# Two more pairs of gate chunks by seven products, and the turn of the merged sums moved behind them

## The chip, the cores and the metric

The kernel runs on one core of one Trainium2 chip. The metric is the device time of one execution in microseconds; for the kernel before it is 2109.54 us, the median of three runs (2108.2 to 2111.12).

## What is computed

Two transformer-like blocks follow each other on 256 tokens of width 2048, in float32. The change lies in the first block, behind its four attention branches. With `x` normalised to `h`, and `p = h @ w_in`, each branch b has a part `z_b` (512 columns) and a gate `g_b` (2048 columns) of `p`:

```
for b in range(4):
    y = branches[b] * silu(z_parts[b])                    # 256 x 512
    term = sigmoid(g_parts[b]) * (y @ w_branch[b])        # 256 x 2048
    merged = term if merged is None else merged + term
x = x + merged @ w_out                                    # the output projection
```

So there are 16 chunks of gates (four branches, four chunks of 512 columns), each a product of h (256 x 2048) with a 2048 x 512 block of `w_in`, and 16 products of y (256 x 512) with a 512 x 512 block of `w_branch`. Then the merged sums, turned, go into four chunks of the output projection.

## The kernel before, in words

**Products.** Every number is split into a high and a low part of 32 bits with a short mantissa, and a product of two numbers is three products on TensorE: high times low, high times high, low times high (`product`, L248 to L252; in the pairs L344). Every product instruction is 128 x 128 by 128 x 512, and adds up in a bank of PSUM.

**Units.** The work is a list of units (`self.units`). A unit is one load of 1 MB of weights (four blocks of 128 rows by 512 columns) with what is done with it: 24 product instructions for a plain unit (four blocks, two halves of the tokens, three products). A chunk of gates is four such units, a branch product is one. `run_units` (L279) writes the program out in order: for unit j it issues the conversion (ScalarE casts the load to `hi`, L317; VectorE subtracts to get `lo`, L318), then the products of unit q = j - 2 with what closes them, then it calls `pump`, then the loads that have become possible. `hi` and `lo` have three buffers, so the cast for unit q + 2 goes into the buffer of unit q - 1. A unit marked `late` has its conversion behind the products of unit q.

**Helpers.** Smaller work is in lists of generators: `pump` (L192) makes one step of the first generator of the list `fast` and of the first of `slow`, once per unit. A generator has to be at the head of its list to be stepped. A unit that needs a result calls `need`, which finishes the generators of that list up to the one named, on the spot. Turning a 256 x 512 part of the sums is such a helper:

```
    def turn_gen(self, src, k0, dst, scale=None):
        yield
        self.turn(src, 4, k0, dst(), scale)
```

Its first step does nothing; the second issues eight transposes on TensorE (L491), and for each of two banks a cast on ScalarE (L507) and a subtraction on VectorE (L508), which give the high and the low part. Unit gi of each chunk of the output projection needs turn ("m", gi).

**Pairs.** Two chunks of gates can go as a pair (`pair_units`, L329): the first eight blocks of x and the two weights are taken as 2 x 2 blocks, and seven products of sums of blocks take the place of eight; the last eight blocks go in plain units (l0, l1, r0, r1). The sums of weight blocks are added by VectorE in the loads' own buffers (L298), and the sums of x's blocks are made once (`forms_of`, L458, two steps, each two additions, four differences, four casts and four subtractions). `weave` puts pairs behind each other in the order of `GATE_PLAN`; r0 and r1 belong to the pair before (for the first pair they are the last two units of the chunk before), and bl and br are the two branch units of the pair before:

```
    order=("P1", "r0", "r1", "P5", "bl", "P6", "P3", "P7", "l0", "Q4", "l1", "P2", "br"),
```

Before, chunk (0,0) and chunk (0,1) go one by one, then five pairs hold (0,2) to (2,3), and the four chunks of branch 3 go one by one, each with a branch unit of an earlier chunk behind its first unit or behind itself. At the end stand branch units (3,2) and (3,3), and then the output projection.

**Places.** At the end of chunk (0,0) `to_merge` (L1006) closes the attention's pools and opens those of the merge, also `pS`, which holds the sums of x's blocks and two more buffers for loads. With the first unit of chunk (0,1) `fresh` (L922) reopens the banks of PSUM as five and three in place of four and four (`banks`, L593) and queues the sums of x's blocks. With the first unit of chunk (3,0) `to_sums` (L1018) closes `pS` and puts the turned sums `mT` in its place; `windows` tells the planner of loads between which units the two more buffers exist. At the end of branch unit (3,c) the turn ("m", c) is queued (L898).

Of the kernel before, what the change touches and what calls it, by code (L numbers as in the profile page):

```python
# [9 lines left out]
F32 = mybir.dt.float32  # L10
# [7 lines left out]
P = 128  # L18
# [3 lines left out]
NB = 4  # L22
BW = 512
FF = 5632
CH = 512
# [150 lines left out]
class Kernel:  # L176
# [413 lines left out]
            self.right.close()  # L590
            self.ps.close()

    def banks(self, n):  # L593

        if n != 4:
            self.ps.close()
        self.ps = ExitStack()
        self.psM = self.ps.enter_context(self.tc.tile_pool(name="psM", bufs=n, space=PSUM))
        self.psA = self.ps.enter_context(self.tc.tile_pool(name="psA", bufs=8 - n, space=PSUM))

    def start(self):

# [157 lines left out]
    def first_block_units(self):  # L760
# [112 lines left out]
        def g_evac(b, c):  # L873
            def evac(ps):
                if (b, c) == (0, 0):
                    self.to_merge()
                for m in range(2):
                    s = sig[b, c, m] = self.p2.tile([P, CH], F32, tag="sig", name="sig", bufs=4)
                    nc.scalar.activation(out=s, in_=ps[m], func=AF.Sigmoid, scale=self.r0(m))
                if (b, c) == (0, 0):  # L880
                    for i in range(2):
                        self.add(self.y_turn(i), name=("y", i))

            return evac

        def b_evac(b, c):
            def evac(ps):
                for m in range(2):
                    r = self.R[:, m, c * CH : (c + 1) * CH]
                    if b == 0:  # L890
                        nc.vector.tensor_tensor(out=r, in0=ps[m], in1=sig[b, c, m], op=ALU.mult)
                    else:
                        t = self.p2.tile([P, CH], F32, tag="tm", name="tm", bufs=2)
                        nc.vector.tensor_tensor(out=t, in0=ps[m], in1=sig[b, c, m], op=ALU.mult)  # L894
                        nc.vector.tensor_tensor(out=r, in0=r, in1=t, op=ALU.add)
                if c == 3 and b < 2:
                    self.add(self.y_turn(b + 2), name=("y", b + 2))
                if b == 3:  # L898
                    self.add(self.turn_gen(lambda m: self.R[:, m, c * CH : (c + 1) * CH], 4 * c, lambda: self.mT), name=("m", c))

            return evac

# [5 lines left out]
        def gate(b, c, fresh=None):  # L908
            return self.gemm(wg(b, c), kx, xl, g_evac(b, c), fresh=fresh)

        def branch(b, c):
            return self.gemm(wb[b, c], k4, lambda: self.yT[b], b_evac(b, c), need=lambda gi: ("y", b), add=False, bank=self.bank)
# [6 lines left out]

            return part  # L920

        def fresh():  # L922
            self.banks(5)
            self.add(self.forms_of(self.xT, forms), slow=True, name="gforms")

        forms = {}
        gate(0, 0)
        first = gate(0, 1, fresh)[0]
        twos = [(b, c) for b in range(3) for c in (0, 2)][1:]
        pairs = [  # L930
            self.pair_units(wg(b, c), wg(b, c + 1), xl, lambda: forms, g_evac(b, c), right_evac(b, c + 1), "gforms" if n == 0 else None)
            for n, (b, c) in enumerate(twos)
        ]
        more = [(branch(b, c)[0], branch(b, c + 1)[0]) for b, c in [(0, 0)] + twos]
        self.weave(pairs, GATE_PLAN, more)
        self.units.append(more[-1][0])
        stop = gate(3, 0, self.to_sums)[0]
        self.units.append(more[-1][1])
        self.windows = [(first, stop)]
        for c in range(4):  # L940
            if c < 3:
                gate(3, c + 1)
            self.units += branch(3, c)


        def o_evac(c):
# [59 lines left out]
    def to_merge(self):  # L1006

        self.drain(self.fast)
        self.drain(self.slow)
        self.left1.close()  # L1010
        tc = self.tc
        self.p2 = self.left.enter_context(tc.tile_pool(name="p2", bufs=1))
        pR = self.right.enter_context(tc.tile_pool(name="pR", bufs=1, side="right"))
        self.R = pR.tile([P, 2, D], F32, name="R")
        self.wide = ExitStack()
        self.pS = self.wide.enter_context(tc.tile_pool(name="pS", bufs=1, side="right"))

    def to_sums(self):  # L1018

        self.wide.close()  # L1020
        self.pB = self.right.enter_context(self.tc.tile_pool(name="pB", bufs=1, side="right"))
        self.mT = self.new_B()

    def to_out(self):

        self.left.close()
        nc, a = self.nc, self.a
        self.left = ExitStack()
        self.p3 = self.left.enter_context(self.tc.tile_pool(name="p3", bufs=1))
        self.xr = self.p3.tile([P, 2, D], F32, name="xr")  # L1030
        self.fw = self.p3.tile([P, D], F32, name="fw")
        nc.gpsimd.dma_start(out=self.xr, in_=a["x"][0].rearrange("(m p) d -> p m d", p=P))
        nc.gpsimd.dma_start(out=self.fw, in_=a["final_norm_w"][None, :].to_broadcast([P, D]))
# [677 lines left out]
```

## Time and profile before

| | |
|---|---|
| time, median of three runs | 2109.54 us (2108.2 to 2111.12) |
| time of the profiled execution | 2108.53 us |
| its span, first to last instruction | 2106.8 us |
| mean granted clock of TensorE | 0.996 |
| TensorE busy with products | 99% of the span, 9412 instructions |
| VectorE, ScalarE busy | 67%, 49% |
| moved by DMA | 401.69 MB, 191 GB/s over the span |

A unit is told from the profile by its place: within the gates, products into `mm` belong to chunks, products into `at` from `yT` to branch units, and transposes into `at` from `R` to the turns of the sums. The gates' first sigmoids are at 491.56 us; the output projection (products from `xB`) begins at 912.15 us. A row of the timeline gives start, duration, engine, line, operation, the tile written and read, the count, and in brackets the idle time before it with what ended it.

### The profile page before, as it was taken

The numbers are of one execution on the slowest core, as the hardware profiler recorded it, in microseconds if no ns is written. First come the engines' busy times: TensorE is split into PE (matmuls) and PEld (weight loads), VectorE is DVE, ScalarE is ACT, GpSimd is POOL, SyncE is SP. The second block draws the span as 40 slices with busy tenths as digits, with TensorE's granted clock in tenths as the row PEclk, the third lists the DMA queues.
The fourth block names the chain that finished last, engine by engine and source line by source line (L and its number), as shares of the span: only waits on it lengthen the run. The fifth ranks groups of instructions, "written<-read, shape, count | busy, mean of one in ns | idle before, by whom it ended". The sixth has DMA issues, their size and how long they took to land.

```text
span 2106.8 us, 22884 instructions
## 1 busy us (share of the span) xinstructions
PE 2079.1 (99%) x9412; PEld 1714.0 (81%) x9412; DVE 1416.8 (67%) x1175; ACT 1033.7 (49%) x975; POOL 36.3 (2%) x65
## 2 busy tenths in 40 slices
PE   8999999998999999999999999999999999999998
PEld 6888888887788888888888888888888888888886
DVE  6457465556788875556589656796578965796554
ACT  5444444444555553445454454555356543555543
POOL 1100000000000000000100000000000000000000
PEclk9999999999999999999999999999999999999999
DMA  7844344454555555565655455446544565456453
GB/s 262 265 158 167 136 172 168 168 192 160 200 200 200 200 185 195 182 237 185 235 180 196 144 200 210 170 180 252 187 180 180 183 252 184 160 184 240 170 180 130
DMA packets 59129, 401.69 MB, mean 191 GB/s; under 512 B 6788, under 2 KB 7440, under 8 KB 12304
## 3 DMA queue, kind: packets, MB, share of 16 engines
q1 hardware_dynamic: 56592, 388.69, 50.5%
q0 software_dynamic: 2288, 11.43, 1.8%
q8 instruction: 74, 1.21, 0.2%
q14 instruction: 31, 0.25, 0.0%
q10 hardware_dynamic: 144, 0.11, 0.0%
HBM read 398.08 MB, written 4.47 MB: 191 GB/s over the span
## 4 chain that ended last, share of the span: by engine, by line
PE 88%; DVE 7%; ACT 2%; issue 2%; DMA 1%; SPq 0%; ACTq 0%; POOLq 0%; POOL 0%; DVEq 0%
PE mm L344 22%; PE mm L250 19%; PE mm L252 19%; PE mm L251 19%; DVE lo L318 4%; PE at L491 2%; ACT hi L317 2%; DVE raw L298 2%; PE at L250 1%; PE at L251 1%; PE at L252 1%; DMA raw<-in_t_w_in_dram 1%; PE at L706 0%; PE at L1085 0%; DVE tm L894 0%
## 5 line engine op out<-in xcount | busy, mean ns | idle before, releaser
L318 DVE TENSOR_TENSOR lo<-raw,hi 128x2048 fp32r<-128x2048 f32 (+3 forms) x420 | 940.4, 2249 | 506.2 <-ACT hi L317 505.2
L317 ACT CAST hi<-raw 128x2048 fp32r<-128x2048 f32 (+3 forms) x420 | 785.0, 1875 | 565.4 <-PE mm L252 293.1
L250 PE MATMUL mm<-lo,xA 128*128 128x512 f32 x1216 | 483.0, 397 | 9.8 <-DVE lo L318 7.8
L252 PE MATMUL mm<-hi,xA 128*128 128x512 f32 x1216 | 476.8, 392 | 0.0
L251 PE MATMUL mm<-hi,xA 128*128 128x512 f32 x1216 | 476.5, 392 | 0.0
L344 PE MATMUL mm<-hi,xA 128*128 128x512 f32 x1320 | 407.2, 390 | 0.0
L344 PEld LDWEIGHTS mm<-hi,xA 128*128 128x128 f32 x1320 | 247.8, 188 | 51.6
L250 PEld LDWEIGHTS mm<-lo,xA 128*128 128x128 f32 x1216 | 230.0, 189 | 59.9 <-DVE lo L318 8.8
L252 PEld LDWEIGHTS mm<-hi,xA 128*128 128x128 f32 x1216 | 230.1, 189 | 48.7
L251 PEld LDWEIGHTS mm<-hi,xA 128*128 128x128 f32 x1216 | 230.4, 190 | 47.0
L344 PE MATMUL mm<-lo,xA 128*128 128x512 f32 x660 | 258.2, 391 | 0.0
L250 PE MATMUL mm<-lo,xB 128*128 128x512 f32 x608 | 240.2, 395 | 0.0
L252 PE MATMUL mm<-hi,xB 128*128 128x512 f32 x608 | 238.6, 392 | 0.0
L251 PE MATMUL mm<-hi,xB 128*128 128x512 f32 x608 | 236.9, 390 | 0.0
L344 PE MATMUL mm<-hi,forms 128*128 128x512 f32 x480 | 150.0, 394 | 0.0
L344 PEld LDWEIGHTS mm<-lo,xA 128*128 128x128 f32 x660 | 123.9, 188 | 27.0 <-DVE lo L318 0.9
L298 DVE TENSOR_TENSOR raw<-raw 128x2048 f32<-128x2048 f32 x60 | 137.3, 2288 | 0.9
L252 PEld LDWEIGHTS mm<-hi,xB 128*128 128x128 f32 x608 | 114.2, 188 | 25.9
L251 PEld LDWEIGHTS mm<-hi,xB 128*128 128x128 f32 x608 | 114.2, 188 | 24.8
L250 PEld LDWEIGHTS mm<-lo,xB 128*128 128x128 f32 x608 | 114.3, 188 | 23.2
L344 PEld LDWEIGHTS mm<-hi,forms 128*128 128x128 f32 x480 | 90.4, 188 | 20.4
L344 PE MATMUL mm<-lo,forms 128*128 128x512 f32 x240 | 95.8, 399 | 3.5 <-issue 2.2
(284 smaller groups left out, 1225.7 us busy)
## 6 DMA issues: line engine op xcount, KB each, us to landing
raw<-in_t_w_in_dram SPq DMA_DIRECT2D x164, 1024.0 KB, 4.8
raw<-in_t_w_gate_dram SPq DMA_DIRECT2D x44, 1024.0 KB, 4.8
raw<-in_t_w_up_dram SPq DMA_DIRECT2D x44, 1024.0 KB, 4.8
raw<-in_t_w_down_dram SPq DMA_DIRECT2D x44, 1024.0 KB, 4.8
raw<-in_t_w_out_dram SPq DMA_DIRECT2D x32, 1024.0 KB, 4.8
raw<-in_t_w_branch_dram SPq DMA_DIRECT2D x16, 1024.0 KB, 4.8
raw<-in_t_w_ple_gate_dram SPq DMA_DIRECT2D x16, 1024.0 KB, 5.1
raw<-in_t_w_in_dram SPq DMA_DIRECT2D x6, 512.0 KB, 7.3
```

Of the source, the lines that this page charges most:

```text
L250: nc.tensor.matmul(ps, xh[:, k, ts], lo, start=first, stop=False)
L251: nc.tensor.matmul(ps, xh[:, k, ts], hi, start=False, stop=False)
L252: nc.tensor.matmul(ps, xl[:, k, ts], hi, start=False, stop=last)
L298: nc.vector.tensor_tensor(out=x.flat(), in0=x.flat(), in1=y.flat(), op=ALU.add)
L317: nc.scalar.copy(out=hi[:, o], in_=vv[:, o])
L318: nc.vector.tensor_tensor(out=lo[:, o], in0=vv[:, o], in1=hi[:, o].bitcast(F32), op=ALU.subtract)
L344: nc.tensor.matmul(st[key], x_[:, k, :], w_[:, k, :], start=first and k + i == 0, stop=k == 3 and i == 2, skip_group_check=True)
L491: self.nc.tensor.transpose(out, in_, self.ident[: in_.shape[0], : in_.shape[0]])
```

## The change

Branch 3's gates become two more pairs, so that seven pairs hold (0,2) to (3,3). The sums of x's blocks are queued in `to_merge`, at the end of chunk (0,0), and no longer with the first unit of chunk (0,1). When the banks are reopened, three tiles are asked for and not used. `to_sums` is called with branch unit (3,2), the last but one ahead of the output projection; it queues the turns of sums 0 and 1, and the ends of branch units (3,2) and (3,3) queue those of 2 and 3.

```
-    def banks(self, n):
+    def banks(self, n, skip=0):
...
+        for _ in range(skip):
+            self.psM.tile([P, CH], F32, tag="mm", name="mm")
...
-                if b == 3:
-                    self.add(self.turn_gen(lambda m: self.R[:, m, c * CH : (c + 1) * CH], 4 * c, lambda: self.mT), name=("m", c))
+                if b == 3 and c > 1:
+                    self.turn_sum(c)
...
-        def fresh():
-            self.banks(5)
-            self.add(self.forms_of(self.xT, forms), slow=True, name="gforms")
-
-        forms = {}
+        def after(f, fn):
+            def both(hi, lo):
+                f()
+                fn(hi, lo)
+
+            return both
+
+        forms = self.gforms = {}
         gate(0, 0)
-        first = gate(0, 1, fresh)[0]
-        twos = [(b, c) for b in range(3) for c in (0, 2)][1:]
+        first = gate(0, 1, lambda: self.banks(5, 3))[0]
+        twos = [(b, c) for b in range(NB) for c in (0, 2)][1:]
...
         self.weave(pairs, GATE_PLAN, more)
-        self.units.append(more[-1][0])
-        stop = gate(3, 0, self.to_sums)[0]
-        self.units.append(more[-1][1])
+        stop = more[-1][0]
+        stop.fn = after(self.to_sums, stop.fn)
+        self.units += more[-1]
         self.windows = [(first, stop)]
-        for c in range(4):
-            if c < 3:
-                gate(3, c + 1)
-            self.units += branch(3, c)
...
         self.pS = self.wide.enter_context(tc.tile_pool(name="pS", bufs=1, side="right"))
+        self.add(self.forms_of(self.xT, self.gforms), slow=True, name="gforms")
...
         self.mT = self.new_B()
+        self.turn_sum(0)
+        self.turn_sum(1)
+
+    def turn_sum(self, c):
+        self.add(self.turn_gen(lambda m: self.R[:, m, c * CH : (c + 1) * CH], 4 * c, lambda: self.mT), name=("m", c))
```

## Rows read from the trace of the kernel before

**Rows 1.** The page, part 1: engine, busy us, share of the span, instructions.

```profile
PE 2079.1 (99%) x9412; PEld 1714.0 (81%) x9412; DVE 1416.8 (67%) x1175; ACT 1033.7 (49%) x975; POOL 36.3 (2%) x65
```

**Rows 2.** The page, part 4: the chain of waits by engine.

```profile
PE 88%; DVE 7%; ACT 2%; issue 2%; DMA 1%; SPq 0%; ACTq 0%; POOLq 0%; POOL 0%; DVEq 0%
```

**Rows 3.** TensorE's waits, 480 to 960 us: us in total, times, longest.

```profile
PE mm L344 <- issue: 2.2, 1, 2.2
PE mm L250 <- ACT sig L879: 2.0, 1, 2.0
...
PE mm L344 <- DVE lo L318: 0.6, 3, 0.2
```

**Rows 4.** Stretches (length, busy by engine, clock): three pairs, branch 3's gates, slow clock.

```profile
582.14:741.57 159.43, 159.03 (x702) 129.75 (x700) 133.07 (x82) 89.48 (x67) 0.00 (x0) 1.00 0.53 198
788.94:900.20 111.26, 111.26 (x497) 91.84 (x496) 59.40 (x41) 45.50 (x33) 0.00 (x0) 1.00 0.53 189
...
493.63:497.04 3.41, 3.41 (x9) 2.66 (x9) 2.29 (x1) 0.99 (x1) 0.00 (x0) 0.50 1.02 430
```

**Rows 5.** Timeline (start, us, instruction, [idle before]), 490 to 530 us.

```profile
491.56 1.27 ACT L879 ACTIVATE sig<-mm,rs 128x512 f32<-128x512 f32 x2
...
492.88 0.50 PE L250 MATMUL mm<-lo,xA 128*128 128x512 f32 x1 [2.01 <-ACT sig L879]
...
517.46 0.50 PE L250 MATMUL mm<-lo,xA 128*128 128x512 f32 x1 [1.65 <-DVE lo L318]
...
525.43 0.47 PE L344 MATMUL mm<-lo,forms 128*128 128x512 f32 x1 [2.24 <-issue]
...
529.91 0.50 PE L250 MATMUL at<-lo,yT 128*128 128x512 f32 x1 [1.49 <-DVE lo L318]
```

**Rows 6.** Timeline of VectorE and ScalarE, 494 to 524 us.

```profile
494.65 2.29 DVE L318 TENSOR_TENSOR lo<-raw,hi 128x2048 fp32r<-128x2048 f32 x1 [4.94 <-ACT hi L317]
...
502.57 1.29 DVE L470 TENSOR_TENSOR fx<-xA 128x512 f32<-128x512 f32 x2
...
507.73 2.29 DVE L318 TENSOR_TENSOR lo<-raw,hi 128x2048 fp32r<-128x2048 f32 x1 [0.95 <-ACT hi L317]
509.94 1.29 DVE L470 TENSOR_TENSOR fx<-xA 128x512 f32<-128x512 f32 x2
...
512.74 1.42 DVE L483 TENSOR_TENSOR forms<-fs,forms 128x256 fp32r<-128x256 f32 x4
515.11 2.29 DVE L318 TENSOR_TENSOR lo<-raw,hi 128x2048 fp32r<-128x2048 f32 x1 [0.95 <-ACT hi L317]
517.32 4.61 DVE L298 TENSOR_TENSOR raw<-raw 128x2048 f32<-128x2048 f32 x2
...
522.55 1.37 ACT L879 ACTIVATE sig<-mm,rs 128x512 f32<-128x512 f32 x2 [0.94 <-PE mm L252]
```

**Rows 7.** Timeline, 911 to 926 us: turns of the sums, first units of the projection.

```profile
911.36 1.04 PE L491 MATMUL at<-ident,R 128*128 128x128 f32 x8
...
912.15 0.47 PE L250 MATMUL mm<-lo,xB 128*128 128x512 f32 x1
...
912.70 0.39 PE L252 MATMUL mm<-hi,xB 128*128 128x512 f32 x1
...
913.53 1.28 DVE L508 TENSOR_TENSOR xB<-at,xB 128x512 fp32r<-128x512 f32 x2
...
917.94 1.91 ACT L317 CAST hi<-raw 128x2048 fp32r<-128x2048 f32 x1 [3.05 <-PE mm L252]
...
919.88 2.29 DVE L318 TENSOR_TENSOR lo<-raw,hi 128x2048 fp32r<-128x2048 f32 x1 [2.67 <-ACT hi L317]
...
923.23 1.04 PE L491 MATMUL at<-ident,R 128*128 128x128 f32 x8
923.87 1.07 ACT L507 CAST xB<-at 128x512 fp32r<-128x512 f32 x2 [4.02 <-PE at L491]
...
924.49 1.29 DVE L508 TENSOR_TENSOR xB<-at,xB 128x512 fp32r<-128x512 f32 x2 [2.32 <-ACT xB L507]
```

## The prediction

> **What bounds the kernel now.** I read the page's busy times first: TensorE is busy for 2079.1 of 2106.8 us, VectorE for 67% [rows 1]. The chain of waits says the same: 88% of the span is TensorE, 7% VectorE [rows 2]. So a change pays by the products that it takes away, and costs by the time in which TensorE then waits. The waits of TensorE between 480 and 960 us come next: apart from four near the start of the gates (below) only three of 0.2 us are left, behind VectorE's subtraction `lo`; no transfer is in the list [rows 3]. Then the stretches: the granted clock is 1.00 (2.4 GHz) in the pairs and in the gates of the fourth branch [rows 4].
>
> **The gates of the fourth branch.** Two chunks one by one are 8 units of 24 products, 192; as a pair they are seven products of blocks with 12 each and four plain units with 24, 180. Both come with two branch units. Measured, from [rows 4]: three pairs with their branches and two transposing turns of y took 159.43 us; a turn is 0.79 us on TensorE (911.36 to 912.15 in [rows 7]), so a pair is (159.43 - 1.58) / 3 = 52.62 us. Four gates with four branches and two turns took 111.26 us, so two gates with two branches are (111.26 - 1.58) / 2 = 54.84 us, and a unit of 24 products is 5.48 us, a product 0.228. A pair saves 2.22 us, two pairs **4.4 us**. By products alone it would be 24 x 0.228 = 5.5; the difference is what TensorE loses to VectorE in a pair, which VectorE fills to 133.07 / 159.43 = 83% (53% in the gates). VectorE's added sums and subtractions lie beside TensorE, with that loss already in the 52.62. If the last two pairs lost 0.3 us more each, 3.8 would be left. The weights loaded stay the same (ten loads of 1 MB for two chunks with their branches in either form), and no transfer holds TensorE in the pairs, so I put the transfers at nothing.
>
> **The sums of x's blocks, at a chunk's end.** The two halves of this step are now issued one unit earlier each. A half is 4.2 us on VectorE (509.94 to 512.74 + 1.42 in [rows 6]) and four casts on ScalarE. Before, the second half stands between the subtraction at 507.73, which r0 needs, and the one at 515.11, which r1 needs. After, the first half falls behind the chunk's two sigmoids, into the time when VectorE sat idle for 4.94 us ahead of 494.65; the second takes the first one's old place at 502.6, and 509.94 comes free. It pushes the conversion for P1 back by ScalarE's casts, about 1.6 us, to 494.65 + 2.29 + 1.6 = 498.5; P1 starts two units behind 492.88, past 503: nothing. Then in order: r1's cast follows r0's at once, its subtraction runs 510.0 to 512.3, so r1 starts at 517.46 - 1.65 = 515.8 without its wait [rows 5] and ends at 521.3. The two sums behind r1 (4.61 us) end at 516.9, the copies of y's turn (1.28) at 518.2, P5's subtraction (2.29) at 520.5: P5 starts at 521.3, and its 2.24 us of waiting go too. Now the sigmoids are late: they are issued ahead of the next branch unit's conversion and end 0.7 us after r1 (522.55 + 1.37 against 525.43 - 2.24), so 522.0, the cast 523.9, the subtraction 526.2. The branch unit starts there and not at 529.91. **Gain 3.7 us**; bounds 0 (all of it is eaten elsewhere) and 5.4 (all three waits of 1.65, 2.24 and 1.49 go).
>
> **The banks passed over.** The three buffers asked for are written by nothing; the pool still has five, and a pair needs four in turn. The wait that it could touch is the 2.01 us before 492.88, with the half clock behind it: 493.63 to 497.04 at 0.50 (1.2 GHz), products 0.43 us apart in place of 0.228, so 3.41 x (1 - 0.228 / 0.425) = 1.6 us [rows 4, 5]. The first product writes one bank, but starts when both sigmoids have ended (491.56 + 1.27), and each of them reads a bank of its own. I read that as a wait of the reopened pool for all users of the closed one, which passing banks over doesn't shorten. I take **0**; bounds -3.6 and 0 (it issues no instruction).
>
> **The sums transposed behind.** Before, the turn of chunk c was issued at the end of branch unit (3,c), and m2's at 911.36 is the last ahead of the output projection. After, m0 and m1 are queued only when branch unit (3,2) begins, m2 and m3 at the ends of the last two branch units. One call of the helper list is made per unit, a turn needs two, and the list is first in, first out: m0 is turned just behind the last branch unit, m1 has had its empty first step when the projection's second unit asks for it, and so have m2 and m3 for the third and fourth unit. So four turns stand right in front of the units that read them; the same 4 x 0.79 us of TensorE as before, but nothing lies between a turn and its reader.
> What this costs is read from [rows 7]. First unit: it would begin as at 912.15, its third product (912.70) reads the low part, which VectorE writes from 913.53 on, 0.64 us for the first bank, behind the four operations that close the branch unit: 914.2, so 1.5 us. Second unit: ahead of the turn's copies ScalarE's queue holds the cast for two units on, which waits until the first unit has left its buffer: 917.94 to 919.86; VectorE's holds the subtraction that follows it, 919.88 to 922.17. Only then comes the low part, 922.8. Without the wait the third product would run at 912.15 + 5.48 + 0.79 + 0.55 = 918.9. So 3.9 us, and the same in the third and fourth unit, since each cast waits for the unit just ended. **1.5 + 3 x 3.9 = 13.2 us**. Bounds: below, the copies run right behind the transposes as at 923.23 (VectorE 924.49, first bank at 925.13, third product at 924.6), 0.6 each; above, 4.9 each (1.92 + 2.29 + 0.65, nothing beside it).
> **The clock.** Of the four waits in [rows 5] one, of 2.01 us, was followed by a stretch at 1.2 GHz. The new ones are twice as long, so I take it to fall behind the three long ones, at 1.1 us each, since part of the slow stretch lies in the wait: **3.3 us**, bounds 0 and 4 x 1.6 = 6.4. In the Trainium skill, "TensorE: Matmul & The Clock Gate", section "HAM oscillation", a kernel that waits between its bursts begins every burst at half rate. By that rule all four stalls would pay 1.6 and the sum would be 3.1 us higher; the trace agrees in one wait of four.
>
> **Sum**, against the profiled execution: its span is 2106.8 us and its time 2108.53, 1.0 below the median of 2109.54, so I set the sum on the median. -4.4 - 3.7 + 0 + 13.2 + 3.3 = +8.4: **2118 us**. With the low ends of the gains' terms and no clock loss, -5.5 - 5.4 + 13.2 = +2.3 (2112); with the high ends -3.8 + 1.5 + 14.7 + 6.4 = +18.8 (2128).
>
> **Rivals.**
> *The copies don't stand behind the conversion* (faster). Place: the second to fourth unit of the projection. Price 0.6 in place of 3.9 us a turn, no clock loss: -4.4 - 3.7 + 1.5 + 1.8 = -4.8, 2104.7. It decides from (8.1 - 1.5) / 3 = 2.2 us a turn downwards. For it: at 923.87 the copies did start 0.64 us after the transposes. Against it: there the turn was issued behind a unit, ahead of the next conversion, and here behind that conversion; and casts do wait for the end of a unit (the idle time before 917.94 is put down to TensorE). 12%.
> *Passing over the banks frees the first product* at 492.88: -3.6 more, 2114.3. For it: the wait's length, and that the second of the sigmoids may read the very bank that comes first. By the Trainium skill, "PSUM — Partial Sum Buffer", section "Specifications (TRN2)", engines may work in PSUM side by side as long as they don't meet in a bank, so the chip itself would not ask for the wait. Against it: both sigmoids were waited for. 10%, and 3% that both rivals hold (2101).
> *Every stall starts the clock low*: +11.5, 2121. 10%.
> *My forecast*: 65%, its own range 2112 to 2124.
>
> **How the numbers follow.** A measurement of this kernel can tell about 0.2%, 4.2 us, from no change. The two cases with hidden copies, 15%, lie at 2101 to 2105, partly within it: faster 0.11. The lower tail of the forecast and of the banks case (below 2113.7) gives, with them, same 0.13. Slower 0.76. The range 2109 to 2125 leaves out the hidden copies and some 4% above.
>
> **What would show it.** Right: waits of TensorE of about 4 us, three times, each behind eight transposes of R and released by VectorE's low part of xB; half clock there; about 52.6 us from branch to branch in the two new pairs; no wait at r1 and P5, one of about 2 us at the first branch unit; the 2 us behind the two sigmoids unchanged. Wrong: no wait in the projection's first chunk (first rival), the first product of the second chunk starting before the sigmoids end (second), pairs above 54 us, or a transfer in the list of TensorE's waits.

## The result and the profile after

The changed kernel takes **2119.84 us** (median of six, 2116.01 to 2123.71), the kernel before 2108.85 (median of six, the three of the table of the time before among them): a ratio of **1.0053, interval 1.0043 to 1.0063**, 11.0 us slower. The forecast was 2118.0, its range 2109 to 2125. The profiled execution is the quickest of the six, 2116.01 us with a span of 2114.0, 7.2 us longer than the span before.

The page of the kernel after, parts 1 and 4, against [rows 1, 2]:

```profile
PE 2075.9 (98%) x9388; PEld 1708.7 (81%) x9388; DVE 1448.7 (69%) x1193; ACT 1047.5 (50%) x989; POOL 37.7 (2%) x65
...
PE 86%; DVE 8%; issue 2%; ACT 2%; DMA 1%; SPq 0%; ACTq 0%; POOLq 0%; POOL 0%; DVEq 0%
```

TensorE has 24 products fewer and is busy 3.2 us less, in a span that is 7.2 us longer: it waits some 10 us more. Its waits between 480 and 960 us (us in total, times, longest) answer to [rows 3]:

```profile
PE mm L252 <- DVE xB L508: 6.0, 4, 1.7
PE mm L250 <- ACT xB L507: 5.1, 4, 1.6
PE at L250 <- DVE lo L318: 2.2, 1, 2.2
PE mm L250 <- ACT sig L881: 2.0, 1, 2.0
PE mm L344 <- DVE lo L318: 1.0, 4, 0.3
```

The first two rows are new: four times a product waits for ScalarE's copy `xB` of the transposed sums and another for VectorE's low part. The third is the wait that the forecast left at the first branch unit, and r1's and P5's are gone. The fourth is the one behind the two sigmoids, unchanged. The second unit of the output projection shows how a new wait comes about (timeline of the kernel after; start, us, instruction, idle time before it):

```profile
907.80 1.03 PE L491 MATMUL at<-ident,R 128*128 128x128 f32 x8
908.00 1.90 ACT L317 CAST hi<-raw 128x2048 fp32r<-128x2048 f32 x1 [4.68 <-PE mm L252]
909.80 1.07 ACT L507 CAST xB<-at 128x512 fp32r<-128x512 f32 x2
909.93 2.29 DVE L318 TENSOR_TENSOR lo<-raw,hi 128x2048 fp32r<-128x2048 f32 x1 [4.29 <-ACT hi L317]
910.43 0.51 PE L250 MATMUL mm<-lo,xB 128*128 128x512 f32 x1 [1.60 <-ACT xB L507]
912.14 1.28 DVE L508 TENSOR_TENSOR xB<-at,xB 128x512 fp32r<-128x512 f32 x2
912.88 0.80 PE L252 MATMUL mm<-hi,xB 128*128 128x512 f32 x1 [1.71 <-DVE xB L508]
```

Read it down the queues. The sums are transposed at 907.80; ScalarE then does the conversion for a later unit, which had waited for the unit just ended (line 317, released by TensorE's last product), and only then the copy (line 507). VectorE does the same: the subtraction of that conversion, then the low part. With nothing in the way the third product would run at 907.80 + 0.79 + 0.55 = 909.14 (the spacing of [rows 7]); it runs at 912.88, **3.74 us late**. In the first unit, reckoned in the same way, it is 1.55 us late (902.64 against 901.09).

Stretches of the kernel after (length, busy us of PE, PEld, DVE, ACT and POOL, then the granted clock, the share of the DMA engines and GB/s):

```profile
492.49:524.12 31.63, 29.47 (x137) 24.13 (x137) 26.10 (x27) 18.10 (x23) 0.00 (x0) 1.00 0.36 143
...
735.73:841.16 105.43, 104.88 (x457) 85.59 (x457) 89.24 (x55) 58.16 (x42) 0.00 (x0) 1.00 0.53 200
...
901.08:947.80 46.72, 35.96 (x144) 27.67 (x145) 17.51 (x18) 14.60 (x20) 1.35 (x2) 0.89 0.45 174
...
911.42:918.25 6.83, 5.38 (x13) 4.23 (x14) 2.00 (x3) 0.00 (x0) 0.00 (x0) 0.50 0.85 355
...
925.07:928.49 3.42, 2.91 (x7) 2.33 (x8) 1.06 (x2) 0.00 (x0) 0.00 (x0) 0.50 0.71 244
```

and the two of the kernel before that answer to the first and the third:

```profile
492.88:529.91 37.03, 31.66 (x136) 25.13 (x137) 28.73 (x33) 18.14 (x22) 0.00 (x0) 0.95 0.32 124
...
912.15:940.61 28.46, 28.46 (x132) 23.41 (x131) 15.76 (x15) 13.19 (x17) 1.35 (x2) 1.00 0.74 288
```

From these the 7.2 us come together. Gates' first product to the first branch unit: 37.03 to 31.63, that is -3.8 by the waits and -1.6 because no half clock follows the sigmoids in this execution. The last two pairs with their branches: 105.43, 52.7 each; the whole gate stage is 4.2 shorter. The projection's first chunk: 46.72 against 28.46, less two turns that now lie inside it (1.58), and its first product 0.54 late: +17.2, of which the four waits are 1.55 + 3 x 3.74 = 12.8 and the half clock, as what is left, the other 4.4 (the products that ran at half clock are 0.427 us apart in place of 0.228, which alone makes 3.9). With 0.4 less up to the gates: -0.4 - 3.8 - 1.6 - 4.2 + 17.2 = +7.2.

### The profile page after: what moved, and what is told of

It is laid out like the page before. It is cut to its first block, busy times and chain, and to the rows that moved or that the text cites. A ratio compares the mean times of both kernels' runs of the same rounds, so it can differ in the third digit from the quotient of the medians.

```text
span 2114.0 us, 22879 instructions
## 1 busy us (share of the span) xinstructions
PE 2075.9 (98%) x9388; PEld 1708.7 (81%) x9388; DVE 1448.7 (69%) x1193; ACT 1047.5 (50%) x989; POOL 37.7 (2%) x65
## 4 chain that ended last, share of the span: by engine, by line
PE 86%; DVE 8%; issue 2%; ACT 2%; DMA 1%; SPq 0%; ACTq 0%; POOLq 0%; POOL 0%; DVEq 0%
PE mm L344 25%; PE mm L252 18%; PE mm L250 18%; PE mm L251 18%; DVE lo L318 5%; ACT hi L317 2%; PE at L491 2%; DVE raw L298 1%; PE at L250 1%; PE at L251 1%; PE at L252 1%; DMA raw<-in_t_w_in_dram 1%; DVE tm L896 0%; PE at L708 0%; PE at L1092 0%
## 5 line engine op out<-in xcount | busy, mean ns | idle before, releaser
L318 DVE TENSOR_TENSOR lo<-raw,hi 128x2048 fp32r<-128x2048 f32 (+3 forms) x426 | 952.6, 2247 | 489.5 <-ACT hi L317 488.6
L317 ACT CAST hi<-raw 128x2048 fp32r<-128x2048 f32 (+3 forms) x426 | 795.0, 1874 | 565.3 <-PE mm L252 275.5
L344 PE MATMUL mm<-hi,xA 128*128 128x512 f32 x1496 | 461.5, 390 | 0.0
L250 PE MATMUL mm<-lo,xA 128*128 128x512 f32 x1088 | 431.3, 396 | 10.1 <-DVE lo L318 8.0
L252 PE MATMUL mm<-hi,xA 128*128 128x512 f32 x1088 | 425.1, 391 | 0.0
L251 PE MATMUL mm<-hi,xA 128*128 128x512 f32 x1088 | 424.9, 390 | 0.0
L344 PEld LDWEIGHTS mm<-hi,xA 128*128 128x128 f32 x1496 | 280.9, 188 | 58.6
L344 PE MATMUL mm<-lo,xA 128*128 128x512 f32 x748 | 292.4, 391 | 0.0
L250 PEld LDWEIGHTS mm<-lo,xA 128*128 128x128 f32 x1088 | 205.0, 188 | 54.5 <-DVE lo L318 9.2
L252 PEld LDWEIGHTS mm<-hi,xA 128*128 128x128 f32 x1088 | 205.1, 188 | 43.4
L251 PEld LDWEIGHTS mm<-hi,xA 128*128 128x128 f32 x1088 | 205.3, 189 | 41.8
L344 PE MATMUL mm<-hi,forms 128*128 128x512 f32 x544 | 169.8, 393 | 0.0
L344 PEld LDWEIGHTS mm<-lo,xA 128*128 128x128 f32 x748 | 140.4, 188 | 30.4 <-DVE lo L318 0.8
L298 DVE TENSOR_TENSOR raw<-raw 128x2048 f32<-128x2048 f32 x68 | 155.6, 2288 | 1.1
L344 PEld LDWEIGHTS mm<-hi,forms 128*128 128x128 f32 x544 | 102.4, 188 | 23.0
L344 PE MATMUL mm<-lo,forms 128*128 128x512 f32 x272 | 108.5, 399 | 1.8 <-DVE lo L318 1.0
```

Of the source, the lines that this page charges most:

```text
L250: nc.tensor.matmul(ps, xh[:, k, ts], lo, start=first, stop=False)
L251: nc.tensor.matmul(ps, xh[:, k, ts], hi, start=False, stop=False)
L252: nc.tensor.matmul(ps, xl[:, k, ts], hi, start=False, stop=last)
L298: nc.vector.tensor_tensor(out=x.flat(), in0=x.flat(), in1=y.flat(), op=ALU.add)
L317: nc.scalar.copy(out=hi[:, o], in_=vv[:, o])
L318: nc.vector.tensor_tensor(out=lo[:, o], in0=vv[:, o], in1=hi[:, o].bitcast(F32), op=ALU.subtract)
```

## The experiments

My theory: the late turns cost 13 us of waiting and some half clock on top, and the other parts are gains that they swallow. Its rivals: the pairs or the earlier sums are at fault, or the wait is one for the transposes themselves and not for the conversion ahead of the copies. Each kernel ran beside the kernel before on one chip, in five rounds.

**e2_turns_late_only: the kernel before, with only the order of the turns changed.**

```diff
-                if b == 3:
-                    self.add(self.turn_gen(...), name=("m", c))
+                if b == 3 and c > 1:
+                    self.turn_sum(c)
...
+            us = branch(3, c)
+            if c == 2:
+                us[0].fn = after(lambda: (self.turn_sum(0), self.turn_sum(1)), us[0].fn)
```

> The kernel before, its gates of branch 3 one by one, but the turns of sums 0 and 1 are queued at the start of branch unit (3,2) and those of 2 and 3 at the ends of the last two branch units; nothing else is changed. Theory (late turns stand right in front of the units that read them, their copies behind the conversion for two units on): four waits of TensorE in the projection's first chunk, 1.5 and three of 3.7 to 3.9 us, 13 us, and with two or three stretches at 1.2 GHz 16 to 18: about 2125 us. Rival (the waits come from the two new pairs, which load VectorE to 83%, and from the sums' place being opened late, not from the turns' order): under 5 us, 2109 to 2114.

Measured: 2128.02 us, ratio 1.0085 (1.0069 to 1.0101), 19.9 above the kernel before. Its waits of TensorE have the new pair of rows and the old ones of the start:

```profile
PE mm L252 <- DVE xB L508: 6.0, 4, 1.7
PE mm L250 <- ACT xB L507: 5.0, 4, 1.6
PE mm L344 <- issue: 2.2, 1, 2.2
```

So the order alone makes the whole loss, with no pair in the fourth branch's gates. By the medians e2 less the kernel after is 8.2 us, near the 4.2 and 3.8 of the other two parts; since the clocks of the two differ from execution to execution, that is agreement and no measurement. Its stretches at half clock in the projection:

```profile
924.40:927.81 3.41, 3.41 (x10) 2.63 (x9) 0.13 (x1) 0.00 (x0) 0.00 (x0) 0.50 1.01 423
934.64:941.47 6.83, 5.62 (x13) 4.46 (x14) 1.75 (x3) 0.00 (x0) 0.00 (x0) 0.50 0.47 156
948.22:951.63 3.41, 2.98 (x7) 2.40 (x8) 0.98 (x2) 0.00 (x0) 0.00 (x0) 0.51 0.73 250
```

One follows each of the three long waits, and the middle one is twice as long: four times 3.41 us, where the kernel after had three. The profiled span is 19.9 us above that before: 1.2 of it lies ahead of the gates (their first sigmoids are at 492.77 against 491.56), 12.8 are the waits, reckoned as above, and some 6 are left for the four stretches, 1.5 each. One of the six executions, with a mean clock of 0.998 against 0.992 and 0.993 in the others, took 2117.81 us, and that is 12.8 more than the one execution of the kernel before at 0.998 in these rounds (2104.97): the waits, nearly bare of the clock.

**e1_sums_of_x_late: the kernel after, with the sums of x's blocks put back.**

```diff
+        def fresh():
+            self.banks(5, 3)
+            self.add(self.forms_of(self.xT, forms), slow=True, name="gforms")
...
-        first = gate(0, 1, lambda: self.banks(5, 3))[0]
+        first = gate(0, 1, fresh)[0]
...
-        self.add(self.forms_of(self.xT, self.gforms), slow=True, name="gforms")
```

> The changed kernel, but the sums of x's blocks are queued with the first unit of chunk (0,1) again, as before; all else as changed. Theory (the second half of these sums, standing between the conversions of r0 and r1, held TensorE three times): 3.7 us slower than the changed kernel, so about 2123.5 us, with waits of TensorE at r1 and P5 of about 1.7 and 2.2 us back and the one at the first branch unit at 1.5. Rival (VectorE's load in this stretch is what counts, wherever the sums are issued; time lost at one unit is made up at the next): within 1 us of the changed kernel.

Measured: 2121.52 us, 1.006 (1.0044 to 1.0076). The three waits of [rows 5] are back, at r1, P5 and the first branch unit:

```profile
PE mm L344 <- issue: 2.2, 1, 2.2
PE mm L250 <- DVE lo L318: 1.6, 1, 1.6
...
PE at L250 <- DVE lo L318: 1.5, 1, 1.5
```

The mechanism is shown, the size is not: 1.7 us above the kernel after, where the kernel after spreads over 7.7 us and e1 over 8.9. e7 and e9, below, measure it.

**e3_no_empty_step: the kernel after, with a turn done in the first step of its helper**, so one unit ahead of its reader.

```diff
     def turn_sum(self, c):
-        self.add(self.turn_gen(...), name=("m", c))
+        def gen():
+            self.turn(lambda m: self.R[:, m, c * CH : (c + 1) * CH], 4, 4 * c, self.mT)
+            return
+            yield
+        self.add(gen(), name=("m", c))
```

> The changed kernel, but the turn of a sum is done in the helper's first step, without the empty one: m0 behind branch unit (3,2), m1 behind (3,3), m2 and m3 behind the projection's first and second unit, so that one unit lies between each turn and its reader. Theory: the 13.2 us of waits and the slow clock behind them go; m0's turn and the last branch unit may meet in the three banks that both use, at most 2.5 us. So 2103 to 2106 us, faster than the kernel before by 3 to 6. Rival (the turned sums' place waits for all users of the place that it takes, which is closed only with branch unit (3,2)): the waits stay at 8 us or more, over 2114.

Measured: 2105.33 us, 0.9983 (0.9974 to 0.9991), 14.5 below the kernel after. No product waits for `xB` in the projection; of TensorE's waits there remain

```profile
PE at L250 <- DVE lo L318: 2.2, 1, 2.2
PE mm L250 <- ACT sig L881: 2.0, 1, 2.0
...
PE at L250 <- DVE tm L896: 0.7, 1, 0.7
PE at L250 <- DVE xB L508: 0.4, 1, 0.4
```

(the last two are m0's turn, which now needs banks while a branch unit is being closed). The same stretch of time that held the waits in the kernel after has none here, at the full clock:

```profile
901.08:947.80 46.72, 46.72 (x222) 38.73 (x221) 27.76 (x26) 22.37 (x26) 1.35 (x2) 1.00 0.62 235
```

The profiled execution is the second quickest of eleven (2100.54 us at a mean clock of 0.997; most of the others are at 0.995), so no trace shows where those lose some 5 us.

**e4_turn_ahead_of_conversion: the turn stays right ahead of its reader, but the conversion is issued behind it.**

```diff
+            us = self.gemm(wo[c], ...)
+            for u in ((us[3],), (us[0], us[1]), (), ())[c]:
+                u.late = True
```

> The changed kernel with one difference of order: for the second, third and fourth unit of the projection the products (and so the turn that they ask for) are issued ahead of the conversion for two units on, not behind it. The turns still stand right in front of their readers. Theory (the price of a turn is the cast and the subtraction that stand ahead of its copies): each of the three waits falls from 3.8 to about 0.6 to 1.2 us, no stretch at 1.2 GHz is left but by chance: 10 to 14 us faster than the changed kernel, 2106 to 2110. Rival (a turn right in front of its reader costs what it costs, transposes, casts and subtractions in a row): waits of 2.5 us or more each, less than 5 us won.

Measured: 2107.18 us, 0.9994 (0.9986 to 1.0003). The same unit as above, in its timeline:

```profile
906.50 1.04 PE L491 MATMUL at<-ident,R 128*128 128x128 f32 x8
907.13 1.08 ACT L507 CAST xB<-at 128x512 fp32r<-128x512 f32 x2 [5.13 <-PE at L491]
907.75 1.29 DVE L508 TENSOR_TENSOR xB<-at,xB 128x512 fp32r<-128x512 f32 x2 [3.42 <-ACT xB L507]
908.09 1.92 ACT L317 CAST hi<-raw 128x2048 fp32r<-128x2048 f32 x1
```

The copies now start 0.63 us after the transposes and the conversion behind them. The third product is 0.66 us late (908.50 against 907.84) in place of 3.74. So it is what stands ahead of the copies in two queues, and not the distance from transposes to reader, that costs 3 of the 3.7 us. (The edit also makes the second chunk's second unit wait 2.2 us, at 936.77, since its conversion now stands behind what closes the first chunk.)

**e6_waits_by_bank: e3, with buffers of the reopened pools that wait each for its own last user**, and without the three buffers passed over. Whether these are asked for or not, the program is the same instruction for instruction, waits and addresses too, and only names of buffers differ; so that part alone cannot change a time, and it has no run of its own.

```diff
-        self.psM = ...tile_pool(name="psM", bufs=n, space=PSUM)
+        self.psM = ...tile_pool(name="psM", bufs=n, space=PSUM, reuse_waits="tile")
...
-        first = gate(0, 1, lambda: self.banks(5, 3))[0]
+        first = gate(0, 1, lambda: self.banks(5))[0]
```

> The kernel of e3 with the reopened banks of PSUM waiting for the users of their own bank alone, not for all users of the banks that were closed; the three unused tiles are left out. Theory (the 2.0 us of TensorE behind the two sigmoids at the end of chunk (0,0) is a wait of the whole reopened pool, so passing over tiles could not touch it): the wait is gone, 2.0 us, and the half clock that follows it in some executions: 2 to 3.6 us faster than e3, 2102 to 2103.5. Rival (the chunk's first product lands on the bank that the second sigmoid reads): the wait stays, and the time is that of e3.

Measured: 2100.51 us, 0.9964 (0.9951 to 0.9978), 4.8 below e3 by the medians, where 2 to 3.6 were expected. The 2.0 us behind the sigmoids are gone from the list, and a wait of 0.5 for `lo` stands there instead: they were a wait of the pool for all users of the closed ones, as read in the prediction. What makes up the rest of the 4.8 is not shown: the two profiled spans, e3's that of a quick execution, are only 0.2 apart (2098.6 and 2098.8).

**e7_sums_of_x_late: e3 with the sums of x's blocks put back** (e1's edit).

> The kernel of e3 with the sums of x's blocks queued with the first unit of chunk (0,1) again, so that their place is tried without the waits and the clock of the projection. Theory: 3.2 to 3.7 us slower than e3, about 2109; waits of 1.7, 2.2 and 1.5 us in place of one of 2.2. Rival (made up later, since VectorE is ahead again by the next pair): within 1 us of e3.

Measured: 2106.53 us, 0.9991 (0.9983 to 1.0): 1.2 above e3 by the medians where about 4 was expected. Most of e3's executions show a mean clock of 0.995 and e7's spread from 0.995 to 0.997, so the clock stands between them, and these medians did not settle the size. The profiled executions do. The first line is e3, the second e7, each from the first sigmoid at the end of chunk (0,0) to the first branch unit:

```profile
491.42:524.37 32.95, 29.47 (x136) 24.13 (x137) 27.01 (x30) 19.43 (x25) 0.00 (x0) 1.00 0.39 156
492.98:531.28 38.30, 31.63 (x137) 25.15 (x137) 28.74 (x33) 19.45 (x24) 0.00 (x0) 0.96 0.35 134
```

They are 5.35 us apart; 1.6 of that is the half clock that follows e7's sigmoids and not e3's, at the price of [rows 4], and 3.75 is left for the step.

**e8_four_waits_less: e6, with the first branch unit's conversion issued ahead of the two sigmoids that close chunk (0,1), not behind them, and m0's turn in banks of the products' pool.**

```diff
-                own[k].late = True
+                own[k].late = not (more and n == 0 and k == "bl")
...
+            bank = (lambda: self.psM.tile([P, CH], F32, tag="mm", name="mm")) if c == 0 else None
...
```

> The kernel of e6 with two more edits: m0's turn takes its two banks from the five of the chunks, not from the three that the last branch units use, and the first pair's branch unit is converted ahead of the sigmoids of chunk (0,1), not behind them. Theory: the 0.7 and 0.4 us that the last branch unit waits for banks go, and the 2.2 us at the first branch unit; with e6's 2.0 this is 5 to 6 us below e3: 2099 to 2101. Rival (VectorE is full at the first pair, and the wait only moves to P6 or P3): 2 us less than that, 2102.

Measured: **2097.39 us, 0.9946 (0.9933 to 0.9958)**, the quickest version, below both kernels. All that TensorE still waits for between 480 and 980 us:

```profile
PE mm L344 <- DVE lo L318: 0.9, 4, 0.3
PE at L250 <- DVE lo L318: 0.7, 1, 0.7
PE mm L250 <- DVE lo L318: 0.5, 1, 0.5
```

Its five executions lie within 1.3 us; the kernel after's six spread over 7.7.

**e9_e8_sums_of_x_late: e8 with the sums of x's blocks put back** (e1's edit), and **e10_e8_gates_one_by_one: e8 with the fourth branch's gates one by one** and the turns of the sums where they were, as before the change.

```diff
-        twos = [(b, c) for b in range(NB) for c in (0, 2)][1:]
+        twos = [(b, c) for b in range(3) for c in (0, 2)][1:]
...
+        for c in range(4):
+            if c < 3:
+                gate(3, c + 1)
+            self.units += branch(3, c)
```

> The kernel of e8 with the sums of x's blocks queued with the first unit of chunk (0,1) again. e7 against e3 left the size of this step open: 1.2 us by the medians, 3.8 by the profiles' stretch, while the clock of the executions differed. With e8's fewer waits the clock should be the same in nearly all executions. Theory (the step is worth 3.7 us and e3's median hid it by more stretches at 1.2 GHz): 2100.5 to 2102.5, 3 to 5 us slower than e8. Rival (most of it is made up later): 2098 to 2099.

> The kernel of e8 with branch 3's gates one by one and the turns of the sums as in the kernel before: the two pairs alone are undone. Theory (a pair is 2.2 us shorter than two gates with the same branch units): 4.4 us slower than e8, 2101 to 2102.5. Rival (the pairs' saving is given back in VectorE's load around the last units and the projection's start): within 2 us of e8, under 2099.5.

Measured: e9 2101.61 us, 0.9967 (0.9955 to 0.998), 4.2 above e8; e10 2100.45 us, 0.9963 (0.995 to 0.9977), 3.1 above e8 (3.6 by the ratios). So both parts are gains, near the size that the prediction gave them, 3.7 and 4.4. Neither median is the step alone. In e8 only 0.7 us of waiting is left at the first branch unit, where the kernel after has 2.2, so the sums had more to win there. And e10's executions are at mean clocks of 0.997 and 0.998, e8's at 0.996 and 0.997, so the medians make the pairs look smaller; in e8's profile a stretch at half clock lies at 242 us, ahead of all that was changed, and in e10's none does. The profiled executions of e8 and e10, from the first branch unit to the projection's first product, are both at the full clock:

```profile
523.14:900.39 377.25, 376.17 (x1652) 307.23 (x1653) 309.61 (x191) 206.11 (x153) 0.00 (x0) 1.00 0.55 198
520.53:902.89 382.36, 381.81 (x1684) 312.82 (x1685) 278.33 (x175) 192.20 (x141) 0.00 (x0) 1.00 0.55 196
```

e8's holds two turns of the sums, e10's three: 382.36 - 377.25 - 0.79 = 4.3 us for the two pairs.

## Why the prediction was right, step by step

**The pairs, -4.4: right.** 52.7 us from pair to pair against 52.62, the gate stage 4.2 shorter; undone alone, 4.3 in the profiles of e10 and e8 (3.1 to 3.6 by their times, at unlike clocks).

**Sums of x's blocks, -3.7: right.** -3.8 in the profile, 3.75 in the profiles of e7 and e3, 4.2 in e9 against e8, and for the reason given: r1 and P5 no longer wait, and the one wait left is where it was put, at the first branch unit (2.2).

**Banks passed over, 0: right.** The first product still waits for both sigmoids (2.0 us), and e6 shows whose wait it is. The rival that these banks would free it falls, and more plainly than the prediction had it: passing over them moves no bank at all. In e6, where the buffers wait one by one, the products run on, 0.23 us apart, beside the two sigmoids (491.18 to 492.45).

**Late turns, +13.2: right.** 1.55 + 3 x 3.74 = 12.8, with the predicted queue order row by row (the sum 918.9 of the prediction is 918.97, which leaves its 3.9 at 3.8). The rival that the copies don't stand behind the conversion falls with the rows at 908.00 and 909.93; e4 shows that its price, 0.6 a turn, is what the other order gives (0.66).

**The clock, +3.3: the mis-sized term.** In the profiles the projection's half clock cost 4.4 us in the kernel after and some 6 in e2. By the medians, 11.0 + 4.2 + 3.8 - 12.8 = 6.2 us is left over, near the upper bound of 6.4. That remainder is not all the price of the new waits: stretches at half clock fall elsewhere too, in the profile before at 240.90 us, where the profile after has none.

```profile
240.90:244.31 3.41, 3.41 (x10) 2.65 (x9) 2.86 (x4) 0.00 (x0) 0.00 (x0) 0.52 0.03 7
```

Two things were off. I priced a stretch at 1.1 us, reasoning that part of it lies in the wait; in both profiled projections 3.41 us of half clock cost 1.5. And I took one stretch behind each of the three long waits; e2 had that, and one of them was a double one of 6.83 us, while the kernel after had a double one, a single one, and none behind the third. The rival by which each stall starts the clock low, 2121, came 1.2 us from the median, my forecast 1.8. The Trainium skill, "TensorE: Matmul & The Clock Gate", section "HAM oscillation", tells of a kernel whose every burst starts at half rate, behind waits of some 3 to 5 us on transfers; the prediction gave that without the length of the waits. The trace of e2 agrees for the three long waits (3.7 us), the kernel after for two of them, and neither shows half clock behind the short wait of 1.55 us. How many stretches fall differs from execution to execution, and the times go with it: the kernel after's at mean clocks of 0.996 and 0.991 took 2116.01 and 2123.71.

The profiled +7.2 looks closer to the forecast's +8.4 than the medians' +11.0 only because that execution was the quickest of its six.

**Open:** what decides in which execution a stretch falls, where it falls in the slower executions of e3, of which there is no trace, and so why e3 and e7 are only 1.2 us apart by their medians and e3 and e6 as much as 4.8.

## What to carry to other kernels

A helper that is issued right in front of its reader pays for everything that already stands in its engines' queues; where that is a conversion waiting for a buffer that the last unit frees, the price was most of its length, 3.7 of 1.9 + 2.3 us, with the engines otherwise half idle. Issue it one unit earlier (no wait left in the projection) or ahead of that conversion (0.7 us). Price a new wait of TensorE with the half clock that follows it, here a third to a half as much again (on 12.8 us, 4.4 in the profile and 6.2 by the medians), and expect the times to spread.

## What the runs showed of the hardware that was not expected

Half clock behind a wait can last twice 3.41 us: 6.83 us at 0.50 after the second unit's wait in the kernel after, and after the third unit's in e2; part of the stretch lies in the wait itself (911.42 to 912.88 in the kernel after). Of three like waits of 3.7 us in one execution two were followed by half clock (the profile after), in e2 all three.
